# Dilated attention in a two-layer decoder trunk: queries sorted by parity and residue, scores in pieces of 32 queries

## The chip, the cores and the metric

The kernel runs on one core of a Trainium2 chip. The metric is the device time of one execution in microseconds (us); lower is better.

## The reference

Two layers, each: x plus half a SwiGLU network; then a mixing block of HGRN2 (a gated linear recurrence) and dilated attention, both gated and added to x; then x plus half of another SwiGLU network. The sequence has 256 positions, the model 1024 features. All is fp32. What the change touches is the attention:

```python
SEQ = 256
ATT_PATTERNS = ((128, 1), (512, 4), (2048, 16))   # window, dilation of three groups
ATT_HEADS = 4
ATT_DH = 128
...
s = jnp.einsum('bhrnqd,bhrnkd->bhrnqk', qb, kb) * (dh ** -0.5)   # keys of the query's residue alone
s = jnp.where(mask, s, -jnp.inf)
lse = jax.nn.logsumexp(s, axis=-1)
p = jnp.exp(s - lse[..., None])
...
alpha = jax.nn.softmax(jnp.stack(lses, axis=0), axis=0)
o_b = jnp.einsum('gbht,gbhtd->bthd', alpha, jnp.stack(outs, axis=0)).reshape(b, t, ATT_OUT)
```

Query t attends to keys t - j x dilation within the window, in each of three groups. The groups are merged by the weights of their denominators, which is one softmax over the keys of all three groups together, with each group's own queries, keys and values. With dilation 4 a query meets only keys of its residue modulo 4, with dilation 16 of its residue modulo 16.

## The kernel before, in words

**Weights.** Nearly all of the work is products with weights. Each weight tile comes from HBM as fp32, is split on ScalarE (ACT, L211 or L258) and VectorE (DVE, L212 or L259) into a high and a low part, and TensorE (PE) multiplies high by high, high by low and low by high. `full` (L240) and `mm_feat` (L216) have the weights as stationary operand and move 256 positions; `wide` (L246) and `mm_half` (L230) have 128 positions as stationary operand and move 512 weight columns, once for positions 0 to 127 and once for 128 to 255. Split weight tiles have four buffers.

**Attention** (`attn`, L550). For three groups g, `qk_unit` makes normalised and rotated queries and keys, transposed to `qT` and `kT` (features on partitions, positions along them). `v_unit` (L594) makes the values `V` (positions on partitions in two halves) by `wide`, scaled by `rstd`, the norm's factor per position. Then, for each of 4 heads:

- `soft` (L599) goes through two halves c of the queries, 128 each; I call this a half head. Scores (L612) are plain fp32 matmuls, one for each group: 128 queries stationary, 128 keys moving for c = 0 and 256 for c = 1, into one PSUM bank or two. DVE adds the mask and takes the maximum (L614), ACT exponentiates with the sum (L617), DVE takes the reciprocal (L618) and scales (L619). PE transposes the probabilities in blocks of 128x128 (L623): 3 for c = 0, 6 for c = 1, and DVE copies them out (L624) to `PT0` (keys 0 to 127) and `PT1` (keys 128 to 255, for the second half of the queries).
- `weigh` (L627) multiplies values by probabilities into one PSUM tile, 3 matmuls of 256 queries (L631) and 3 of 128 (L633), and ACT and DVE split the result into two parts (L635, L636), the input of the next weight product.

**What sets the order.** `HEAD_ORDER` (L26) interleaves scores, values and weighting in the program. A scheduler in the tile framework then puts the instructions of each engine into a fixed order when the program is built, so weight matmuls of other stages stand between a half head's scores and its transposes. Each engine runs its own list strictly in that order. Small PSUM results share three banks.

**Another user of the same form.** HGRN2's `gram` (L432) multiplies with only 32 columns of the array: four neighbouring matmuls write four different strips of 32 PSUM partitions, by `tile_position`. `square_sums` (L275) takes the squares' sums over features by matmuls with a column of ones (L287), and `norm_scale` (L297) makes `rstd` from them.

From the first transposes of probabilities to the last weighting, layer 0 takes 427 to 491 us of the span, layer 1 1123 to 1187.

Of the kernel before, what the change touches and what calls it, by code (L numbers as in the profile page):

```python
# [9 lines left out]
F32 = mybir.dt.float32  # L10
F32R = mybir.dt.float32r
I32 = mybir.dt.int32
AF = mybir.ActivationFunctionType
# [3 lines left out]
T = 256  # L17
# [5 lines left out]
CW = 512  # L23
# [9 lines left out]
LINE = 512  # L33
MOVE, STAND = 32, 108
EPS = 1e-6
BIG = 3.0e38
MIX_HQ, MIX_HF, MIX_HI, MIX_HG = 0, 1024, 2048, 3072
MIX_AQ, MIX_AK, MIX_AV, MIX_GA, MIX_GB = 4096, 5632, 7168, 8704, 9728
# [2 lines left out]
C_ID = 0  # L41
C_COS = 128
C_SIN = 384
C_M0 = 640
C_M1 = C_M0 + 384
C_LV = C_M1 + 768
C_END = C_LV + 8 * 32


def _shape_constants():  # L50

    c = np.zeros((128, C_END), np.float32)
    c[:, C_ID:C_ID + 128] = np.eye(128, dtype=np.float32)
    inv = (10000.0 ** (-np.arange(0, 128, 2) / 128.0)).astype(np.float32)
    ang = np.arange(T, dtype=np.float32)[:, None] * inv[None, :]
    cos, sin = np.cos(ang.astype(np.float64)), np.sin(ang.astype(np.float64))
    for h in range(2):
        r = slice(h * 128, (h + 1) * 128)
        c[:, C_COS + h * 128:C_COS + (h + 1) * 128] = np.concatenate([cos[r], cos[r]], 1)
        c[:, C_SIN + h * 128:C_SIN + (h + 1) * 128] = np.concatenate([-sin[r], sin[r]], 1)  # L60
    for h, base, n in ((0, C_M0, 128), (1, C_M1, 256)):
        t = np.arange(128)[:, None] + 128 * h
        s = np.arange(n)[None, :]
        for g, (w, d) in enumerate(((128, 1), (512, 4), (2048, 16))):
            ok = (t - s >= 0) & (t - s <= w) & ((t - s) % d == 0)
            c[:, base + g * n:base + (g + 1) * n] = np.where(ok, 0.0, -BIG)
    s = (np.arange(128) % 32)[:, None]
    t = np.arange(32)[None, :]
    lv = [(s // 4 == t // 4) & (t - s == d) for d in range(4)]
    lv += [(s // 16 == t // 16) & (t // 4 - s // 4 == d) for d in range(1, 4)]  # L70
    lv += [(s < 16) & (t >= 16)]
    for i, m in enumerate(lv):
        c[:, C_LV + i * 32:C_LV + (i + 1) * 32] = m
    return c


@with_exitstack
def trunk(ctx, tc, x, ffn1_norm, ffn1_w_in, ffn1_w_out, mix_norm, w_in, lb_logits, out_norm,
# [38 lines left out]
    rstd = const.tile([128, 2], F32, name="rstd")  # L117
# [4 lines left out]
    m0 = ct[:, C_M0:C_M0 + 384]  # L122
    m1 = ct[:, C_M1:C_M1 + 768]

    def lv_f(i):
        return ct[:, C_LV + i * 32:C_LV + (i + 1) * 32]
# [100 lines left out]
                nc.tensor.matmul(o, hi[:, f], al, start=False, stop=False, skip_group_check=True)  # L227
                nc.tensor.matmul(o, lo[:, f], ah, start=False, stop=e, skip_group_check=True)  # L228

    def mm_half(o, h, wu, ah, al, k0, nk, first, last):  # L230

        t = slice(h * 128, (h + 1) * 128)
        for k in range(nk):
            hi, lo = wu[k]
            s, e = first and k == 0, last and k == nk - 1
            nc.tensor.matmul(o, ah[:, k0 + k, t], hi, start=s, stop=False, skip_group_check=True)  # L236
            nc.tensor.matmul(o, ah[:, k0 + k, t], lo, start=False, stop=False, skip_group_check=True)  # L237
            nc.tensor.matmul(o, al[:, k0 + k, t], hi, start=False, stop=e, skip_group_check=True)  # L238

    def full(w, col, ap, nk=KD, step=0):  # L240
        wu = unit(w, 0, nk, col, step)
# [1 line left out]
        mm_feat(ps, wu, ap, 0, nk, True, True)  # L243
        return ps

    def wide(w, col, ap, nk=KD):  # L246

        ah, al = halves(ap)
        ps = [ps_mm.tile([128, 512], F32, name="mm") for _ in range(2)]
        for k0 in range(0, nk, 4):  # L250
            raw = wts.tile([128, KD, CU], F32, name="raw", bufs=RB).rearrange("p (k a) c -> p k (a c)", a=2)
            n = min(4, nk - k0)
            nc.sync.dma_start(raw[:, :n, :],
                              w[k0 * 128:(k0 + n) * 128, col:col + CW].rearrange("(k p) c -> p k c", p=128))
            for a in range(0, n, 2):
                hi, lo = weight_parts(MOVE, CW)
                r = raw[:, a:a + 2, :]
                nc.scalar.activation(hi, r, AF.Copy)  # L258
                nc.vector.tensor_sub(lo, r, hi.bitcast(F32))  # L259
                wu = [(hi[:, k, :], lo[:, k, :]) for k in range(2)]  # L260
                for h in range(2):
                    mm_half(ps[h], h, wu, ah, al, k0 + a, 2, k0 + a == 0, k0 + a + 2 == nk)
        return ps

    def v2(a):
# [9 lines left out]
    def square_sums(work):  # L275
        acc = work.tile([128, 2, T], F32, name="nacc", bufs=1)
        for q in range(KD // 2):
            if q == 0:
                nc.scalar.activation(acc, xT[:, 0:2, :], AF.Square)
            else:  # L280
                sq = work.tile([128, 2, T], F32, name="nsq", bufs=2)
                nc.scalar.activation(sq, xT[:, 2 * q:2 * q + 2, :], AF.Square)
                nc.vector.tensor_add(acc, acc, sq)
        nc.vector.tensor_add(acc[:, 0, :], acc[:, 0, :], acc[:, 1, :])
        ps = bank("tr")
        for h in range(2):
            nc.tensor.matmul(ps[:, h:h + 1], acc[:, 0, h * 128:(h + 1) * 128], ones[:, 0:1], start=True, stop=True)  # L287
        return ps[:, 0:2]

    def square_sums_x(work, x0):  # L290
        ss = work.tile([128, 2], F32, name="nss", bufs=1)
# [3 lines left out]
        return ss  # L295

    def norm_scale(work, ss):  # L297
        ms = work.tile([128, 2], F32, name="nms", bufs=1)
        nc.vector.tensor_scalar(ms, ss, 1.0 / D, EPS, op0=OP.mult, op1=OP.add)
        nc.gpsimd.tensor_tensor(rstd, ms, mhalf[:, 0:2], op=OP.pow)  # L300
# [249 lines left out]
    def attn(ap, l, obh, obl):  # L550
# [41 lines left out]
                nc.vector.tensor_copy(dst[:, g, hs, :], pt)  # L592

        def v_unit(g):  # L594
            ps = wide(w, MIX_AV + g * CW, xp)
            for c in range(2):
                nc.scalar.activation(V[:, g, c, :], ps[c], AF.Copy, scale=rstd[:, c:c + 1])

        def soft(h):  # L599
            PT0 = ap.tile([128, 3, T], F32, name="pt0", bufs=2)  # L600
            PT1 = ap.tile([128, 3, 128], F32, name="pt1", bufs=2)
            for c in range(2):
                n = 128 * (c + 1)
                S = ap.tile([128, 3, n], F32, name=f"as{c}", bufs=2)
                mx = ap.tile([128, 4], F32, name=f"amx{c}", bufs=2)
                t = slice(c * 128, (c + 1) * 128)
                mk = (m0, m1)[c].rearrange("p (g s) -> p g s", g=3)
                prev = BIG
                for i, gs in enumerate([(0, 1, 2)] if c == 0 else [(0, 1), (2,)]):
                    sp_ = bank()[:, :len(gs) * n].rearrange("p (g s) -> p g s", s=n)  # L610
                    for j, g in enumerate(gs):
                        nc.tensor.matmul(sp_[:, j, :], qT[:, g, h, t], kT[:, g, h, 0:n], start=True, stop=True)  # L612
                    r = slice(gs[0], gs[-1] + 1)
                    nc.vector.tensor_tensor_reduce(out=S[:, r, :], in0=sp_, in1=mk[:, r, :], scale=-1.0, scalar=prev,  # L614
                                                   op0=OP.add, op1=OP.min, accum_out=mx[:, i:i + 1])
                    prev = mx[:, i:i + 1]
                nc.scalar.activation(S, S, AF.Exp, scale=-1.0, bias=prev, accum_out=mx[:, 2:3])  # L617
                nc.vector.reciprocal(mx[:, 3:4], mx[:, 2:3])  # L618
                nc.vector.tensor_scalar(S, S, mx[:, 3:4], None, op0=OP.mult)  # L619
                for s in range(c + 1):  # L620
                    pt = bank()[:, :384].rearrange("p (g t) -> p g t", g=3)
                    for g in range(3):
                        nc.tensor.transpose(pt[:, g, :], S[:, g, s * 128:(s + 1) * 128], ident)  # L623
                    nc.vector.tensor_copy(PT0[:, :, t] if s == 0 else PT1, pt)  # L624
            return PT0, PT1

        def weigh(h, PT0, PT1):  # L627
            v = slice(h * 128, (h + 1) * 128)
            po = bank()[:, :T]
            for g in range(3):  # L630
                nc.tensor.matmul(po, V[:, g, 0, v], PT0[:, g, :], start=(g == 0), stop=False, skip_group_check=True)  # L631
            for g in range(3):
                nc.tensor.matmul(po[:, 128:256], V[:, g, 1, v], PT1[:, g, :], start=False, stop=(g == 2),  # L633
                                 skip_group_check=True)
            nc.scalar.activation(obh[:, h, :], po, AF.Copy)  # L635
            nc.vector.tensor_sub(obl[:, h, :], po, obh[:, h, :].bitcast(F32))  # L636

        for g in range(3):
            qk_unit(0, MIX_AQ, qT, g)
# [10 lines left out]
    def mix(l):  # L650
        norm_parts(1, l)
        with ExitStack() as es:
            mp = es.enter_context(tc.tile_pool(name="mix", bufs=1))
            pf0 = full(w_in[l], MIX_HF, xp)
            with tc.tile_pool(name="norm", bufs=2) as work:
                norm_scale(work, square_sums(work))
# [90 lines left out]
```

## Time and profile before

| | |
|---|---|
| median of 3 runs | 1410.68 us (1410.31 to 1411.54) |
| the profiled execution | 1410.22 us |
| its span, first to last instruction | 1408.4 us |
| granted TensorE clock, mean | 0.998 |
| busy: PE, PEld, DVE, ACT, POOL | 1398.9, 1324.4, 992.7, 790.2, 92.5 us |
| DMA queue of the weights, share of 16 engines | 53.8% |

PE is TensorE's matmuls, PEld its weight loads, which overlap them. In a row of a group stand the line, engine and operation, output<-input, shapes and count, then busy us and mean ns of one, then idle time before it and what ended that. In a timeline row stand the start, the length up to the last end, and the group; `x6` is six neighbouring instructions. A plain fp32 matmul stands as two instructions. A matmul's own time is longer than the distance to the next one's start, since matmuls are pipelined.

### The profile page before, as it was taken

To read this page: it belongs to the slowest core of one execution; us is meant where nothing else is said; L and a number is where in the kernel's file an instruction comes from. 1 tells how busy PE (TensorE), PEld (TensorE's weight loads), DVE (VectorE), ACT (ScalarE), POOL (GpSimd) and SP (SyncE) were. 2 spreads that over 40 slices of the span, in tenths; PEclk is the share of its full clock that TensorE was granted. 3 is DMA by queue.
4 is the path that set the end of the run, shared out by engine and by line. 5 is a ranking of instruction groups with operands and counts; after the bars stand their busy time and mean duration, and the time that the engine had idled before them with its cause. 6 is when DMAs were issued, how large, how long until landed. Compare 5 with 4: busy or idle time off the path is not lost.

```text
span 1408.4 us, 26973 instructions
## 1 busy us (share of the span) xinstructions
PE 1398.9 (99%) x11362; PEld 1324.4 (94%) x11362; DVE 992.7 (70%) x1452; ACT 790.2 (56%) x1259; POOL 92.5 (7%) x86
## 2 busy tenths in 40 slices
PE   8999999999999999999999999999999999999998
PEld 7999998998889999999999999988988899999987
DVE  6766569876986687666567665798779766777653
ACT  6544457667864565454454544666577646555442
POOL 0000010003510000000000000100035000000000
PEclk9999999999999999999999999999999999999999
DMA  9665564445554365655556555554454534665652
GB/s 303 199 195 187 187 210 151 150 150 180 179 180 150 120 198 192 200 189 193 196 187 202 183 191 195 183 174 139 159 181 155 196 119 143 202 202 188 195 180 104
DMA packets 215882, 253.17 MB, mean 180 GB/s; under 512 B 4225, under 2 KB 182609, under 8 KB 215761
## 3 DMA queue, kind: packets, MB, share of 16 engines
q1 hardware_dynamic: 215584, 251.38, 53.8%
q8 instruction: 89, 1.46, 0.4%
q14 instruction: 33, 0.26, 0.1%
q10 hardware_dynamic: 176, 0.07, 0.0%
HBM read 250.39 MB, written 1.05 MB: 179 GB/s over the span
## 4 chain that ended last, share of the span: by engine, by line
PE 99%; ACT 0%; DMA 0%; DVE 0%; issue 0%
PE mm L226 23%; PE mm L228 23%; PE mm L227 22%; PE mm L236 8%; PE mm L238 8%; PE mm L237 8%; PE sm L432 1%; PE sm L612 1%; PE tr L591 1%; PE sm L631 1%; PE sm L623 1%; PE sm L633 0%; PE sm L497 0%; PE sm L542 0%; PE sm L524 0%; PE sm L523 0%
## 5 line engine op out<-in xcount | busy, mean ns | idle before, releaser
L211 ACT ACTIVATE wp<-raw 128x1024 fp32r<-128x1024 f32 (+1 forms) x354 | 367.8, 1041 | 395.9 <-PE mm L228 309.6
L212 DVE TENSOR_TENSOR wp<-raw,wp 128x1024 fp32r<-128x1024 f32 (+1 forms) x354 | 424.3, 1200 | 230.0 <-ACT wp L211 227.5
L226 PE MATMUL mm<-xp,wp 128*128 128x256 f32 x1920 | 532.3, 278 | 1.8 <-ACT wp L211 1.8
L228 PE MATMUL mm<-xp,wp 128*128 128x256 f32 x1920 | 532.9, 278 | 0.2 <-DVE wp L212 0.2
L227 PE MATMUL mm<-xp,wp 128*128 128x256 f32 x1920 | 532.7, 278 | 0.0
L226 PEld LDWEIGHTS mm<-xp,wp 128*128 128x128 f32 x1920 | 360.9, 188 | 3.3 <-ACT wp L211 2.1
L228 PEld LDWEIGHTS mm<-xp,wp 128*128 128x128 f32 x1920 | 361.1, 188 | 1.1 <-DVE wp L212 0.4
L227 PEld LDWEIGHTS mm<-xp,wp 128*128 128x128 f32 x1920 | 361.0, 188 | 0.6
L259 DVE TENSOR_TENSOR wp<-raw,wp 128x1024 fp32r<-128x1024 f32 x126 | 155.4, 1234 | 64.2 <-ACT wp L258 63.4
L258 ACT ACTIVATE wp<-raw 128x1024 fp32r<-128x1024 f32 x126 | 133.2, 1063 | 80.5 <-PE mm L238 46.3
L236 PE MATMUL mm<-wp,xp 128*128 128x512 f32 x416 | 164.8, 396 | 0.0
L238 PE MATMUL mm<-wp,xp 128*128 128x512 f32 x416 | 163.4, 393 | 0.0
L237 PE MATMUL mm<-wp,xp 128*128 128x512 f32 x416 | 162.9, 392 | 0.0
L226 PE MATMUL mm<-hp,wp 128*128 128x256 f32 x528 | 145.7, 276 | 0.0
L227 PE MATMUL mm<-hp,wp 128*128 128x256 f32 x528 | 145.7, 276 | 0.0
L228 PE MATMUL mm<-hp,wp 128*128 128x256 f32 x528 | 145.7, 276 | 0.0
L226 PEld LDWEIGHTS mm<-hp,wp 128*128 128x128 f32 x528 | 99.1, 188 | 0.0
L228 PEld LDWEIGHTS mm<-hp,wp 128*128 128x128 f32 x528 | 99.1, 188 | 0.0
L227 PEld LDWEIGHTS mm<-hp,wp 128*128 128x128 f32 x528 | 99.1, 188 | 0.0
L238 PEld LDWEIGHTS mm<-wp,xp 128*128 128x128 f32 x416 | 78.2, 188 | 16.2
L236 PEld LDWEIGHTS mm<-wp,xp 128*128 128x128 f32 x416 | 78.2, 188 | 15.4
L237 PEld LDWEIGHTS mm<-wp,xp 128*128 128x128 f32 x416 | 78.2, 188 | 15.3
(194 smaller groups left out, 1741.0 us busy)
## 6 DMA issues: line engine op xcount, KB each, us to landing
raw<-in_ffn_w_in_dram SPq DMA_DIRECT2D x87, 1024.0 KB, 5.1
raw<-in_w_in_dram SPq DMA_DIRECT2D x84, 1024.0 KB, 4.9
raw<-in_ffn_w_out_dram SPq DMA_DIRECT2D x34, 1024.0 KB, 5.1
raw<-in_ffn_w_out_dram SPq DMA_DIRECT2D x12, 768.0 KB, 4.4
raw<-in_w_branch_a_dram SPq DMA_DIRECT2D x8, 1024.0 KB, 5.1
raw<-in_w_out_dram SPq DMA_DIRECT2D x8, 1024.0 KB, 5.7
raw<-in_w_branch_b_dram SPq DMA_DIRECT2D x8, 512.0 KB, 3.4
x<-in_x_dram SPq DMA_DIRECT2D x4, 256.0 KB, 3.9
```

Source lines behind the costliest of these rows:

```text
L211: nc.scalar.activation(hi[:, :n, :], r, AF.Copy)
L212: nc.vector.tensor_sub(lo[:, :n, :], r, hi[:, :n, :].bitcast(F32))
L226: nc.tensor.matmul(o, hi[:, f], ah, start=s, stop=False, skip_group_check=True)
L227: nc.tensor.matmul(o, hi[:, f], al, start=False, stop=False, skip_group_check=True)
L228: nc.tensor.matmul(o, lo[:, f], ah, start=False, stop=e, skip_group_check=True)
L236: nc.tensor.matmul(o, ah[:, k0 + k, t], hi, start=s, stop=False, skip_group_check=True)
L237: nc.tensor.matmul(o, ah[:, k0 + k, t], lo, start=False, stop=False, skip_group_check=True)
L238: nc.tensor.matmul(o, al[:, k0 + k, t], hi, start=False, stop=e, skip_group_check=True)
L258: nc.scalar.activation(hi, r, AF.Copy)
L259: nc.vector.tensor_sub(lo, r, hi.bitcast(F32))
L432: nc.tensor.matmul(p[32 * b:32 * b + 32, c * n:(c + 1) * n], kk[:, o], mov(o), start=True, stop=True, tile_position=(0, 32 * b))
L591: nc.tensor.transpose(pt[:, h, c * 128:(c + 1) * 128], z[:, c, 2 * a + h, :], ident)
```

## The change

A half head c now holds the queries of one parity, t mod 2 = c, in four pieces of 32, each with one residue modulo 8 (`rho`). Its scores are 12 matmuls of 32 array columns, one for each piece and group, written to the piece's own strip of PSUM partitions. A piece meets all 256 keys in the first group, the 64 keys of its residue modulo 4 in the second and the 32 keys of its residue modulo 8 in the third; the masks, in the new order, leave the right ones. Queries are read with a step of 8 elements, keys with a step of 1, 4 and 8. The whole half head fits one bank of 352 columns. The probabilities of the first group are scaled where they are (256 columns); those of the second and third go to blocks of 128x128 that are zero elsewhere (two DVE operations, four ACT copies). Four transposes follow, one copy of 512 columns, and `weigh` has 2 matmuls of 256 queries and 4 of 128. The values of the second and third group are made with positions sorted by parity, so the activations are read with a step of 2 in `mm_half`, and `rstd` gets two more columns. The result is written back to the order of positions by ACT and DVE. The blocks are zeroed on POOL once in a layer.

```diff
-        t = slice(h * 128, (h + 1) * 128)
+    def half_of(a, h, turned):
+
+        return a.rearrange("p (t c) -> p c t", c=2)[:, h, :] if turned else a[:, h * 128:(h + 1) * 128]
...
         for k in range(nk):
+            ahk, alk = (half_of(a[:, k0 + k, :], h, turned) for a in (ah, al))
...
+            nc.tensor.matmul(o, ahk, hi, start=s, stop=False, skip_group_check=True)
+            nc.tensor.matmul(o, ahk, lo, start=False, stop=False, skip_group_check=True)
+            nc.tensor.matmul(o, alk, hi, start=False, stop=e, skip_group_check=True)
...
-        for h in range(2):
-            nc.tensor.matmul(ps[:, h:h + 1], acc[:, 0, h * 128:(h + 1) * 128], ones[:, 0:1], start=True, stop=True)
+        for i in range(4 if turned else 2):
+            nc.tensor.matmul(ps[:, i:i + 1], half_of(acc[:, 0, :], i % 2, i > 1), ones[:, 0:1], start=True, stop=True)
...
+            ps = wide(w, MIX_AV + g * CW, xp, turned=g > 0)
...
+        def every(a, i, n):
+            return a.rearrange("p (t n) -> p n t", n=n)[:, i, :]
+
+        blocks = [[ap.tile([128, 2, 128], F32, name=f"ab{c}{i}", bufs=1) for i in range(2)] for c in range(2)]
+        for a in blocks[0] + blocks[1]:
+            nc.gpsimd.memset(a, 0.0)
...
-                        nc.tensor.matmul(sp_[:, j, :], qT[:, g, h, t], kT[:, g, h, 0:n], start=True, stop=True)
+                for g, n in enumerate((1, 4, 8)):
+                    for j in range(4):
+                        rho = c + 2 * (j // 2) + 4 * (j % 2)
+                        nc.tensor.matmul(sp_[32 * j:32 * j + 32, at:at + T // n], every(qT[:, g, h, :], rho, 8),
+                                         every(kT[:, g, h, :], rho % n, n), start=True, stop=True,
+                                         tile_position=(0, 32 * j))
+                    at += T // n
+                nc.vector.tensor_tensor_reduce(out=S, in0=sp_[:, 0:SC], in1=masks[c], scale=-1.0, scalar=BIG,
+                                               op0=OP.add, op1=OP.min, accum_out=mx[:, 0:1])
+                nc.scalar.activation(S, S, AF.Exp, scale=-1.0, bias=mx[:, 0:1], accum_out=mx[:, 2:3])
                 nc.vector.reciprocal(mx[:, 3:4], mx[:, 2:3])
-                nc.vector.tensor_scalar(S, S, mx[:, 3:4], None, op0=OP.mult)
+                nc.vector.tensor_scalar(S[:, 0:T], S[:, 0:T], mx[:, 3:4], None, op0=OP.mult)
+                for j in range(4):
+                    p = slice(32 * j, 32 * j + 32)
+                    a = j // 2 + 2 * (j % 2)
+                    if j % 2 == 0:
+                        p2 = slice(32 * j, 32 * j + 64)
+                        nc.vector.tensor_scalar(every(B[p2, 0, :], j // 2, 2), S[p2, T:T + 64], mx[p2, 3:4], None,
+                                                op0=OP.mult)
+                    nc.scalar.activation(every(B[p, 1, :], a, 4), S[p, T + 64:SC], AF.Copy, scale=mx[p, 3:4])
+                pt = bank().rearrange("p (g t) -> p g t", g=4)
+                for i in range(4):
+                    src = S[:, i * 128:(i + 1) * 128] if i < 2 else B[:, i - 2, :]
+                    nc.tensor.transpose(pt[:, i, :], src, ident)
+                nc.vector.tensor_copy(PT[:, :, t], pt)
...
+            for s in range(2):
+                nc.tensor.matmul(po, V[:, 0, s, v], PT[:, s, :], start=(s == 0), stop=False, skip_group_check=True)
+            for g in (1, 2):
+                for c in range(2):
+                    t = slice(c * 128, (c + 1) * 128)
+                    nc.tensor.matmul(po[:, t], V[:, g, c, v], PT[:, 1 + g, t], start=False, stop=(g == 2 and c == 1),
+                                     skip_group_check=True)
```

**Where instructions move.** First PE, in layer 0, at the end of head 0 and the start of head 1. Before, the six transposes (`as` is the probabilities, `ct` holds the identity) and the next half head's scores (`kT`, `qT`) stand as two closed groups between weight matmuls (`pp`, `wp`):

```order
L228 MATMUL mm<-pp,wp 128x256
L226 MATMUL mm<-pp,wp 128x256
L623 MATMUL sm<-ct,as_4571 128x128 x6
L612 MATMUL sm<-kT,qT 128x128 x3
L227 MATMUL mm<-pp,wp 128x256
```

Now, at the same place (`ab` is the blocks, rows of 32 are the strips of the array):

```order
L229 MATMUL mm<-pp,wp 128x256
L230 MATMUL mm<-pp,wp 128x256
L649 MATMUL sm<-ct,as_4596 128x128 x2
L629 MATMUL sm<-kT,qT 32x256
L649 MATMUL sm<-ct,ab_3838 128x128 x2
L629 MATMUL sm<-kT,qT 32x256 x3
L629 MATMUL sm<-kT,qT 32x64 x4
L629 MATMUL sm<-kT,qT 32x32 x4
L231 MATMUL mm<-pp,wp 128x256
```

One of the four pieces of the first group moved between the transposes, alone. It is so in five of the eight half heads of each layer; in the first one the third group's pieces stand apart, 100 rows behind the others, and in two the scores stand together.

Then ACT, from the exponentials of head 0's second half to those of head 1 (`av` is the values, `wp<-raw` the split of weights). Before:

```order
L617 ACTIVATE as_4571,amx_4572<-as_4571,amx_4572 128x768
L597 ACTIVATE av<-mm,rstd 128x512
L211 ACTIVATE wp<-raw 128x1024 x2
L617 ACTIVATE as_4799,amx_4800<-as_4799,amx_4800 128x384
L211 ACTIVATE wp<-raw 128x1024 x2
L617 ACTIVATE as_4814,amx_4815<-as_4814,amx_4815 128x768
```

Now:

```order
L635 ACTIVATE as_4596,amx_4597<-as_4596,amx_4597 128x352
L606 ACTIVATE av<-mm,rstd 128x512
L645 ACTIVATE ab_3838<-as_4596,amx_4597 32x32 x4
L606 ACTIVATE av<-mm,rstd 128x512
L214 ACTIVATE wp<-raw 128x1024 x2
L635 ACTIVATE as_4832,amx_4833<-as_4832,amx_4833 128x352
L645 ACTIVATE ab_3837<-as_4832,amx_4833 32x32 x4
L214 ACTIVATE wp<-raw 128x1024 x2
L635 ACTIVATE as_4863,amx_4864<-as_4863,amx_4864 128x352
L645 ACTIVATE ab_3839<-as_4863,amx_4864 32x32 x4
```

The four copies into the blocks stand behind each exponential, most often directly, ahead of the weight splits that followed it before.

More of the change, by code (lines that the diff above doesn't have):

```diff
@@ L35 @@
 EPS = 1e-6
+SC = T + 64 + 32
 BIG = 3.0e38
@@ L58, in _shape_constants @@
         r = slice(h * 128, (h + 1) * 128)
[L59 to L66, printed above, removed]
+        tab[:, C_COS + h * 128:C_COS + (h + 1) * 128] = np.concatenate([cos[r], cos[r]], 1)
+        tab[:, C_SIN + h * 128:C_SIN + (h + 1) * 128] = np.concatenate([-sin[r], sin[r]], 1)
+    row = np.arange(128)
+    for c in range(2):
+        rho = c + 2 * (row // 64) + 4 * (row // 32 % 2)
+        t = (rho + 8 * (row % 32))[:, None]
+        at = C_MK + c * SC
+        for n, (w, d) in zip((1, 4, 8), ((128, 1), (512, 4), (2048, 16))):
+            gap = t - (rho[:, None] % n + n * np.arange(T // n)[None, :])
+            ok = (gap >= 0) & (gap <= w) & (gap % d == 0)
+            tab[:, at:at + T // n] = np.where(ok, 0.0, -BIG)
+            at += T // n
     s = (np.arange(128) % 32)[:, None]
@@ L121, in trunk @@
     sin_t = ct[:, C_SIN:C_SIN + 256].rearrange("p (h d) -> p h d", h=2)
-    m0 = ct[:, C_M0:C_M0 + 384]
-    m1 = ct[:, C_M1:C_M1 + 768]
+    masks = [ct[:, C_MK + c * SC:C_MK + (c + 1) * SC] for c in range(2)]
     def lv_f(i):
@@ L228, in mm_feat, with mm_half @@
                 nc.tensor.matmul(o, lo[:, f], ah, start=False, stop=e, skip_group_check=True)
-    def mm_half(o, h, wu, ah, al, k0, nk, first, last):
-        t = slice(h * 128, (h + 1) * 128)
+    def half_of(a, h, turned):
+        return a.rearrange("p (t c) -> p c t", c=2)[:, h, :] if turned else a[:, h * 128:(h + 1) * 128]
+    def mm_half(o, h, wu, ah, al, k0, nk, first, last, turned=False):
         for k in range(nk):
+            ahk, alk = (half_of(a[:, k0 + k, :], h, turned) for a in (ah, al))
             hi, lo = wu[k]
             s, e = first and k == 0, last and k == nk - 1
-            nc.tensor.matmul(o, ah[:, k0 + k, t], hi, start=s, stop=False, skip_group_check=True)
-            nc.tensor.matmul(o, ah[:, k0 + k, t], lo, start=False, stop=False, skip_group_check=True)
-            nc.tensor.matmul(o, al[:, k0 + k, t], hi, start=False, stop=e, skip_group_check=True)
+            nc.tensor.matmul(o, ahk, hi, start=s, stop=False, skip_group_check=True)
+            nc.tensor.matmul(o, ahk, lo, start=False, stop=False, skip_group_check=True)
+            nc.tensor.matmul(o, alk, hi, start=False, stop=e, skip_group_check=True)
     def full(w, col, ap, nk=KD, step=0):
@@ L244, in full, with wide @@
         return ps
-    def wide(w, col, ap, nk=KD):
+    def wide(w, col, ap, nk=KD, turned=False):
         ah, al = halves(ap)
@@ L261, in wide @@
                 for h in range(2):
-                    mm_half(ps[h], h, wu, ah, al, k0 + a, 2, k0 + a == 0, k0 + a + 2 == nk)
+                    mm_half(ps[h], h, wu, ah, al, k0 + a, 2, k0 + a == 0, k0 + a + 2 == nk, turned)
         return ps
@@ L273, in norm_parts, with square_sums @@
                                            xh[:, k, :].bitcast(F32), op0=OP.mult, op1=OP.subtract)
-    def square_sums(work):
+    def square_sums(work, turned=False):
         acc = work.tile([128, 2, T], F32, name="nacc", bufs=1)
@@ L285, in square_sums @@
         ps = bank("tr")
-        for h in range(2):
-            nc.tensor.matmul(ps[:, h:h + 1], acc[:, 0, h * 128:(h + 1) * 128], ones[:, 0:1], start=True, stop=True)
-        return ps[:, 0:2]
+        for i in range(4 if turned else 2):
+            nc.tensor.matmul(ps[:, i:i + 1], half_of(acc[:, 0, :], i % 2, i > 1), ones[:, 0:1], start=True, stop=True)
+        return ps[:, 0:4 if turned else 2]
     def square_sums_x(work, x0):
@@ L297, in norm_scale @@
     def norm_scale(work, ss):
-        ms = work.tile([128, 2], F32, name="nms", bufs=1)
+        n = ss.shape[1]
+        ms = work.tile([128, n], F32, name="nms", bufs=1)
         nc.vector.tensor_scalar(ms, ss, 1.0 / D, EPS, op0=OP.mult, op1=OP.add)
-        nc.gpsimd.tensor_tensor(rstd, ms, mhalf[:, 0:2], op=OP.pow)
+        nc.gpsimd.tensor_tensor(rstd[:, 0:n], ms, mhalf[:, 0:n], op=OP.pow)
         pr = bank("tr")
@@ L594, in v_unit @@
         def v_unit(g):
[L595 removed]
+            o = 2 if g else 0
+            ps = wide(w, MIX_AV + g * CW, xp, turned=g > 0)
             for c in range(2):
[L597 removed]
+                nc.scalar.activation(V[:, g, c, :], ps[c], AF.Copy, scale=rstd[:, o + c:o + c + 1])
+        def every(a, i, n):
+            return a.rearrange("p (t n) -> p n t", n=n)[:, i, :]
+        blocks = [[ap.tile([128, 2, 128], F32, name=f"ab{c}{i}", bufs=1) for i in range(2)] for c in range(2)]
@@ L599, in soft @@
+        for a in blocks[0] + blocks[1]:
+            nc.gpsimd.memset(a, 0.0)
         def soft(h):
-            PT0 = ap.tile([128, 3, T], F32, name="pt0", bufs=2)
-            PT1 = ap.tile([128, 3, 128], F32, name="pt1", bufs=2)
+            PT = ap.tile([128, 4, T], F32, name="pt", bufs=2)
             for c in range(2):
-                n = 128 * (c + 1)
-                S = ap.tile([128, 3, n], F32, name=f"as{c}", bufs=2)
+                S = ap.tile([128, SC], F32, name=f"as{c}", bufs=2)
+                B = blocks[c][h % 2]
@@ L605, in soft @@
                 mx = ap.tile([128, 4], F32, name=f"amx{c}", bufs=2)
                 t = slice(c * 128, (c + 1) * 128)
[L607 to L624, printed above, removed]
@@ L628, in weigh @@
+                pt = bank().rearrange("p (g t) -> p g t", g=4)
[3 more added lines that the diff above has]
+                nc.vector.tensor_copy(PT[:, :, t], pt)
+            return PT,
+        def weigh(h, PT):
             v = slice(h * 128, (h + 1) * 128)
             po = bank()[:, :T]
-            for g in range(3):
-                nc.tensor.matmul(po, V[:, g, 0, v], PT0[:, g, :], start=(g == 0), stop=False, skip_group_check=True)
@@ L632, in weigh @@
[L632 to L636, printed above, removed]
+            for s in range(2):
+                nc.tensor.matmul(po, V[:, 0, s, v], PT[:, s, :], start=(s == 0), stop=False, skip_group_check=True)
+            for g in (1, 2):
+                for c in range(2):
+                    t = slice(c * 128, (c + 1) * 128)
+                    nc.tensor.matmul(po[:, t], V[:, g, c, v], PT[:, 1 + g, t], start=False, stop=(g == 2 and c == 1),
+                                     skip_group_check=True)
@@ L638, in attn @@
+            for c in range(2):
+                src = po[:, c * 128:(c + 1) * 128].rearrange("p (b u f) -> p b u f", b=2, u=2)
+                dh, dl = (o[:, h, :].rearrange("p (f u b c) -> p c b u f", u=2, b=2, c=2)[:, c] for o in (obh, obl))
+                nc.scalar.activation(dh, src, AF.Copy)
+                nc.vector.tensor_sub(dl, src, dh.bitcast(F32))
         for g in range(3):
@@ L655, in mix @@
             with tc.tile_pool(name="norm", bufs=2) as work:
-                norm_scale(work, square_sums(work))
+                norm_scale(work, square_sums(work, True))
             oap = parts_of(mp, KD, "pp")
```

20 lines of the change are left out of this document (10 added, 10 removed).

## Prediction

> **What bounds the kernel now.** I read the page's busy times first, then its chain of waits, then the busy time by stretches of the span.
>
> ```profile
> span 1408.4 us, 26973 instructions
> PE 1398.9 (99%) x11362; PEld 1324.4 (94%) x11362; DVE 992.7 (70%) x1452; ACT 790.2 (56%) x1259; POOL 92.5 (7%) x86
> PE 99%; ACT 0%; DMA 0%; DVE 0%; issue 0%
> 432.00:500.00 68.00, 68.00 (x558) 66.88 (x557) 44.80 (x76) 35.80 (x47) 0.00 (x0) 1.00 0.38 124
> 1090.00:1185.00 95.00, 95.00 (x645) 87.53 (x644) 67.71 (x113) 54.95 (x86) 3.29 (x2) 1.00 0.44 148
> ```
>
> TensorE is busy from end to end, and the chain that ended last is 99% PE. The last two rows are stretches that hold most of the attention of layer 0 and of layer 1 (columns: length, then PE, PEld, DVE, ACT and POOL busy, granted clock, DMA): PE never idles there and its clock is full, while DVE has a third and ACT nearly half of its time free. So the change is worth what it adds to or takes from PE's own stream. A busy PE says nothing of rate, so I take prices from the distance between starts in the timeline, below for the last transposes of one head half and the weighting of a head.
>
> ```profile
> 449.88 0.28 PE L227 MATMUL mm<-pp,wp 128*128 128x256 f32 x1
> 449.99 0.28 PE L228 MATMUL mm<-pp,wp 128*128 128x256 f32 x1
> 450.11 0.82 PE L623 MATMUL sm<-ct,as 128*128 128x128 f32 x6
> 450.76 1.46 PE L631 MATMUL sm<-pt,av 128*128 128x256 f32 x6
> 452.06 0.83 PE L633 MATMUL sm<-pt,av 128*128 128x128 f32 x6
> 452.65 0.36 PE L226 MATMUL mm<-pp,wp 128*128 128x256 f32 x1
> 452.85 0.28 PE L227 MATMUL mm<-pp,wp 128*128 128x256 f32 x1
> ```
>
> A weight matmul of 256 columns comes every 0.113 us (449.88 to 449.99 to 450.11). Three plain fp32 matmuls stand as six instructions, so each is two passes. A transpose costs (450.76 - 450.11) / 6 = 0.109, a pass of 256 columns (452.06 - 450.76) / 6 = 0.217, a pass of 128 columns (452.85 - 452.06 - 0.113) / 6 = 0.113. The scores (L612) have the same two shapes and I give them the same prices.
>
> **What the change takes away.** Scores of a head: 3 matmuls of 128 columns and 3 of 256, so 6 x 0.113 + 6 x 0.217 = 1.98 us; 8 heads in two layers: 15.8 us. Transposes: 8 for 9 a head, 8 x 0.109 = 0.9 us less. Weighting: 4 passes of 256 and 8 of 128 (1.77 us) in place of 6 and 6 (1.98), 8 x 0.21 = 1.7 us less.
>
> **What it adds: scores in pieces.** There are now 16 half heads, each with 4 pieces x 3 groups, 32 columns of the array wide, moving 256, 64 and 32 keys. The kernel has such matmuls already, in HGRN2 (L432): four neighbours on four column strips.
>
> ```profile
> 218.76 0.28 PE L227 MATMUL mm<-xp,wp 128*128 128x256 f32 x1
> 218.97 1.08 PE L432 MATMUL sm<-W,hk 128*32 128x128 f32 x32
> 219.98 0.39 PE L228 MATMUL mm<-xp,wp 128*128 128x256 f32 x1
> 220.20 0.28 PE L226 MATMUL mm<-xp,wp 128*128 128x256 f32 x1
> 276.57 0.28 PE L227 MATMUL mm<-xp,wp 128*128 128x256 f32 x1
> 276.78 0.46 PE L432 MATMUL sm<-hqq,s4k 128*32 128x32 f32 x32
> 277.17 0.39 PE L228 MATMUL mm<-xp,wp 128*128 128x256 f32 x1
> 277.39 0.28 PE L226 MATMUL mm<-xp,wp 128*128 128x256 f32 x1
> L432 PE MATMUL sm<-W,hk 128*32 128x128 f32 x256 | 9.7, 276 | 0.0
> L432 PE MATMUL sm<-hqq,s4k 128*32 128x32 f32 x256 | 3.7, 198 | 0.0
> ```
>
> The 32 passes of 128 columns last 1.08 us, of which the last one's own time is 0.28: 0.80 us for seven steps of four passes, less some 0.04 of start, so 0.109 us for four. That is the price of one full-width pass of 128: four strips run side by side. For 32 columns, (0.46 - 0.20 - 0.03) / 7 = 0.034. Between the two, 64 columns are 0.059; 256 columns I take at the full-width 0.217. A half head is then 2 x (0.217 + 0.059 + 0.034) = 0.62 us, and 16 of them 9.9 us.
>
> **The boundaries.** Going into strips and back costs. From 218.76 to 220.20 are 1.44 us: two weight matmuls (0.23), eight steps of 0.109 (0.87), and 0.34 left over. From 276.57 to 277.39: 0.82 - 0.23 - 0.27 = 0.32. So 0.33 for each group of strip matmuls between full-width ones: the entry waits, and the first weight matmul behind has lost the cover for its weight load (0.22 to the next in place of 0.113). The Trainium skill says the same ("TensorEngine Tiling (Array Packing)", Key Properties): changing the tiling mode drains TensorE. It gives no time, so by it alone the sum would stand at the first rival's figure plus a drain without a price for every group.
>
> In the changed order such groups are not 16 but 28: in five of the eight half heads of a layer, one piece is issued alone between transposes, and in the first the third group comes apart, since its keys come later. The same pattern of one strip matmul between transposes stands in layer 1 of the old trace:
>
> ```profile
> 971.09 0.33 PE L542 MATMUL sm<-ct,hog 128*128 128x128 f32 x1
> 971.35 0.41 PE L432 MATMUL sm<-W,hk 128*32 128x128 f32 x2
> 971.68 0.33 PE L542 MATMUL sm<-ct,hog 128*128 128x128 f32 x1
> ```
>
> From transpose to transpose 0.59 us: 0.109 for it, two passes of 0.109, and 0.27 for the boundary. So ten boundaries at 0.27 and eighteen at 0.33 make 8.6 us. And the ten pieces that go alone run their 2 x 0.217 beside nothing, while the other three still take as long as four: 10 x 0.43 = 4.3 us.
>
> Scores so far: 9.9 + 8.6 + 4.3 - 15.8 = +7.0 us.
>
> **Steps in memory.** Queries are read 8 elements apart as stationary operand, keys of the second group 4 apart and of the third 8 apart as moving operand, and the turned values' activations 2 apart. No TensorE operand steps in the trace of before. ACT's do:
>
> ```profile
> L424 ACT ACTIVATE X<-W 128x512 f32<-128x512 f32 x8 | 9.3, 1166 | 2.9 <-DVE W L401 2.0 <-DVE s4B L415 0.9
> L424 ACT ACTIVATE hqq<-X 128x512 f32<-128x512 f32 x8 | 5.0, 625 | 3.2 <-DVE X L401 3.1
> L412 ACT ACTIVATE s1k<-hk 128x128 f32<-128x128 f32 x8 | 3.4, 430 | 0.0
> L412 ACT ACTIVATE s4k<-s1k 128x128 f32<-128x128 f32 x8 | 2.4, 303 | 0.1
> ```
>
> The first of each pair takes single elements 513 or 4 apart, the second runs of four: (1166 - 625) / 512 = 1.06 ns and (430 - 303) / 128 = 0.99 ns more per element. Ends for TensorE: nothing (a plain fp32 pass takes 0.217 / 256 = 0.85 ns a column, which may hide a step), or ACT's 1 ns for the elements of all four strips in turn, 4 x (64 + 32) x 2 passes x 16 = 12.3 us. I take ACT's 1 ns once for the 64 + 32 columns that the strips read side by side, as in the nearest row: 2 x 96 ns = 0.19 us a half head, +3.1 us. The skill's rule on SBUF ("SBUF — State Buffer", Specifications) is that a 16-byte line wants two hits for full bandwidth; the ACT pairs agree with it; by it the second and third group pay, and the fourth rival falls.
>
> The turned values are 192 matmuls with 512 moving columns, whose weight load must fit under the matmul before it:
>
> ```profile
> 393.13 0.39 PE L238 MATMUL mm<-wp,xp 128*128 128x512 f32 x1
> 393.36 0.39 PE L236 MATMUL mm<-wp,xp 128*128 128x512 f32 x1
> L236 PEld LDWEIGHTS mm<-wp,xp 128*128 128x128 f32 x416 | 78.2, 188 | 15.4
> ```
>
> A matmul comes every 0.23 us and the load takes 0.188, so 0.04 is free. With a line shared by two elements the load grows by perhaps a seventh of ACT's 1 ns a column, 0.02 us: hidden. I count zero; without that cover it is the third rival. By the same page's rule two hits a line are enough, so it also says zero.
>
> **Small edits.** Two more sums of squares a layer, each two passes. The row below gives 0.125 us a pass, eight passes: +1.0 us.
>
> ```profile
> L287 PE MATMUL tr<-ones,nacc 128*128 128x1 f32 x20 | 2.5, 228 | 0.0
> ```
>
> Masks of another layout, four memsets on an idle POOL, the power of four columns: off the path, zero. What covers the new ACT and DVE work is the time between scores and transposes:
>
> ```profile
> 436.39 0.72 PE L612 MATMUL sm<-kT,qT 128*128 128x128 f32 x5
> 438.23 0.54 DVE L614 CUSTOM_DVE_ANT_0 as<-sm,ct 128x384 f32<-128x384 f32 x1
> 438.82 0.62 ACT L617 ACTIVATE as<-as,amx 128x384 f32<-128x384 f32 x1 [2.68 <-DVE amx L614]
> 439.71 0.16 DVE L618 RECIPROCAL amx<-amx 128x1 f32<-128x1 f32 x1
> 439.91 0.42 DVE L619 TENSOR_SCALAR as<-as,amx 128x384 f32<-128x384 f32 x1
> 442.54 0.49 PE L623 MATMUL sm<-ct,as 128*128 128x128 f32 x3
> L467 ACT ACTIVATE AT<-ha 32x128 f32<-32x128 f32 x32 | 9.8, 308 | 8.3 <-DVE ha L439 7.3 <-DVE s4S L414 0.8
> ```
>
> The probabilities are ready at 440.33, and PE comes for them at 442.54: 2.2 us of cover. The four copies into the blocks now stand behind the exponential on ACT, wait there for the reciprocal, hold up the next weight cast, and end 4 x 0.31 = 1.2 us after it, at about 441.1. ACT had just waited 2.68 us for work, so the cast has room. Zero; if a cast gets between, up to 1 us a half head (second rival).
>
> **The sum.** +7.0 - 0.9 - 1.7 + 1.0 + 3.1 = +8.5 us. The profiled execution took 1410.22 us (span 1408.4), the median of three runs is 1410.68: 1418.7 by the one, 1419.2 by the other. I say 1419.0.
>
> **Rivals.**
> 1. *Faster: the boundaries are hidden among long passes.* The 28 edges of strip groups cost nothing where a pass lasts 0.217 us, time enough for a weight load of 0.188. Then, with steps free, 9.9 + 4.3 - 15.8 - 0.9 - 1.7 + 1.0 = -3.2 us: 1407.5. It decides where a boundary is 3.2 / 28 = 0.11 us. Against it: no group of strips in the trace pays under 0.27. Chance 0.04.
> 2. *The chain over ACT and DVE becomes late.* Transposes of the blocks then wait in most half heads, 16 x 0.5 us more: 1427. For it: ACT is strictly in order and now waits on DVE twice in a half head. Against it: the 2.2 us. Chance 0.1.
> 3. *The turned weight loads stick out.* At ACT's full 1.06 ns a column they take 0.188 + 0.136 = 0.324 us, 0.095 over the matmul's pace, 192 times: +18 us, 1437. Chance 0.07.
> 4. *Steps cost TensorE nothing.* 1419.0 - 3.1 = 1415.9. For it: the fp32 pass is half as fast as the weight matmuls' (0.217 against 0.113 for 256). Chance 0.22.
> 5. *The pieces don't run side by side with 256 columns*, so that the change doesn't do what it says: 16 x 3 x 0.43 = +21 us, 1440. Against it: the 128-column steps. Chance 0.03.
>
> The forecast itself has 0.54. The range goes from 1413 (steps free, boundaries at 0.23) to 1427 (the second rival, or most of the way to the steps' upper end). 0.2% is 2.8 us, about what a measurement of this kernel can tell from no change: faster by more 0.04, within it 0.07 (steps free and boundaries a third cheaper), slower 0.89.
>
> **What would show it.** In the profile after: PE still 99% busy; the starts within a half head's group 0.2 us apart for four passes of 256; two separate groups per half head in five of eight; about 0.3 us left over at each; the 64- and 32-key steps at about 0.12 and 0.07 us for four if reads step at ACT's price, at 0.06 and 0.03 if they step free. The prediction is wrong if the weight loads of the turned values show more than 0.22 us, if PE shows idle time before the transposes of the blocks, or if boundaries fall below 0.2 us.

## The result and the profile after

| | before | after |
|---|---|---|
| median (range), 6 runs each | 1411.11 us (1409.84 to 1411.72) | 1419.78 us (1418.48 to 1420.34) |
| profiled execution, span | 1410.22, 1408.4 us | 1418.48, 1416.7 us |

The ratio is 1.0062, with a 95% interval from 1.0052 to 1.0072: slower by 0.6%, 8.7 us, where 1419.0 us was forecast.

The page of the profile after has the same picture as before, only longer. Its span, busy times and chain:

```profile
span 1416.7 us, 27633 instructions
PE 1407.5 (99%) x11650; PEld 1323.3 (93%) x11650; DVE 997.0 (70%) x1468; ACT 807.6 (57%) x1327; POOL 91.6 (6%) x94
PE 99%; ACT 0%; DMA 0%; DVE 0%; issue 0%
```

The two stretches with the attention, columns as in the prediction:

```profile
432.00:500.00 68.00, 68.00 (x635) 62.95 (x634) 45.20 (x83) 42.56 (x77) 0.00 (x0) 1.00 0.37 118
1090.00:1185.00 95.00, 95.00 (x735) 82.06 (x734) 65.10 (x119) 59.14 (x116) 3.45 (x3) 1.00 0.45 147
```

And all that PE waited for on other engines in the whole span (us in total, times, longest):

```profile
PE sm L168 <- DMA x<-in_x_dram: 4.0, 1, 4.0
PE mm L229 <- ACT wp L214: 1.7, 1, 1.7
```

PE grew by 8.6 us of busy time and the span by 8.3. ACT grew by 17 us, and PE did not wait for it: both waits of PE lie at the start of the program, none in the attention. In the attention PE is never idle, but its weight loads (PEld) cover less of it than before, 62.95 of 68 us against 66.88, as one would expect of more boundaries. The 8.3 us are inside PE's own stream, so I read them there. First a half head whose scores are split by the transposes, then one whose 24 passes stand together (12 matmuls of two passes; a timeline row bears the shape of its first):

```profile
436.49 0.28 PE L230 MATMUL mm<-pp,wp 128*128 128x256 f32 x1
436.61 0.38 PE L649 MATMUL sm<-ct,as 128*128 128x128 f32 x2
436.92 0.65 PE L629 MATMUL sm<-kT,qT 128*32 128x256 f32 x2
437.50 0.44 PE L649 MATMUL sm<-ct,ab 128*128 128x128 f32 x2
437.87 1.02 PE L629 MATMUL sm<-kT,qT 128*32 128x256 f32 x22
438.82 0.38 PE L231 MATMUL mm<-pp,wp 128*128 128x256 f32 x1
439.04 0.28 PE L229 MATMUL mm<-pp,wp 128*128 128x256 f32 x1
...
454.46 1.03 PE L629 MATMUL sm<-kT,qT 128*32 128x256 f32 x24
455.42 0.38 PE L231 MATMUL mm<-pp,wp 128*128 128x256 f32 x1
455.64 0.28 PE L229 MATMUL mm<-pp,wp 128*128 128x256 f32 x1
```

Together, the 24 passes take 0.96 us to the next weight matmul; split, two and twenty-two take 0.58 and 0.95, so the 22 gain nothing from the two that ran ahead. After each group the next two weight matmuls stand 0.22 apart. I measured every block with scores in both traces in the same way: from the start of the matmul ahead of it to the start of the second weight matmul behind it, less 0.113 for each weight matmul that this counts in (0.2275 where it moves 512 columns), and less the transposes and the weighting at their prices. The scores took 16.1 us before and 26.7 after; the rounding of the prices leaves about 0.1 us open. Below, "by the blocks" means this sum.

### The profile page after: what moved, and what is told of

Its sections match the earlier page's. It is cut to its first block, busy times and chain, and to the rows that moved or that the text cites. A ratio compares the mean times of both kernels' runs of the same rounds, so it can differ in the third digit from the quotient of the medians.

```text
span 1416.7 us, 27633 instructions
## 1 busy us (share of the span) xinstructions
PE 1407.5 (99%) x11650; PEld 1323.3 (93%) x11650; DVE 997.0 (70%) x1468; ACT 807.6 (57%) x1327; POOL 91.6 (6%) x94
## 4 chain that ended last, share of the span: by engine, by line
PE 99%; ACT 0%; DMA 0%; DVE 0%; issue 0%
PE mm L231 23%; PE mm L229 22%; PE mm L230 22%; PE mm L243 8%; PE mm L245 8%; PE mm L244 8%; PE sm L629 2%; PE sm L440 1%; PE tr L599 1%; PE sm L649 1%; PE sm L661 1%; PE sm L657 0%; PE sm L505 0%; PE sm L550 0%; PE sm L533 0%; PE sm L532 0%
```

## The experiments

There were two sessions. Experiments 1, 4, 6 and 7 were timed beside the kernel before, which had 1410.60 us there. The changed kernel itself and experiments 2, 3 and 5 were timed in the other session, where the kernel before had 1410.71 us. Differences below are to the changed kernel's 1419.1 us unless another base is named.

**The base.** No edit.

> The changed kernel itself, as the base for the three runs beside it on this chip: 1419.8 us by every theory.

Measured: 1419.10 us (1418.77 to 1420.23), ratio to before 1.0061 (1.0049 to 1.0074).

**1. Scores of a whole head together.** The two loops over half heads are parted:

```diff
...
+            banks = []
             for c in range(2):
                 sp_ = bank()
...
+                banks.append(sp_)
+            for c in range(2):
...
+                sp_ = banks[c]
                 nc.vector.tensor_tensor_reduce(out=S, in0=sp_[:, 0:SC], in1=masks[c], ...
...
```

> The scores of both half heads of a head are issued before the softmax of either. The program's order then has 12 strip groups in place of 28 and no piece of 256 keys alone between transposes; pieces, steps, transposes and weighting are as in the changed kernel. Theory (boundaries cost about 0.3 each, lone pieces 0.43 each): 16 x 0.29 + 10 x 0.43 = 8.9 us less than the changed kernel, about 1411 us. Rival (boundaries are hidden, only lone pieces cost): 4.3 us less, 1415.5. Rival (neither costs; the pieces themselves are slow): no change. If the transposes now come too early for the softmax, PE shows idle time ahead of them and the gain is smaller.

Measured: 1411.09 us (1410.00 to 1412.02, 11 runs), ratio to before 1.0003 (0.9994 to 1.0012): 8.0 us less. The same 384 passes, with the same steps, and the kernel is back at the time of before. From the same weight matmul at about 56 us to the last one, the traces differ by 9.0 us; the medians also hold the start of the program, which differs by up to 1.5 us among the traces of the changed kernel and its variants. Two half heads in one group, from the timeline:

```profile
433.58 0.40 PE L245 MATMUL mm<-wp,xp 128*128 128x512 f32 x1
433.90 1.83 PE L627 MATMUL sm<-kT,qT 128*32 128x256 f32 x48
435.67 0.39 PE L229 MATMUL mm<-pp,wp 128*128 128x256 f32 x1
435.89 0.28 PE L230 MATMUL mm<-pp,wp 128*128 128x256 f32 x1
```

48 passes in 1.77 us, 0.89 for a half head. Boundaries and lone pieces together are the cost, and the rival by which neither costs falls. This run alone doesn't part the two.

**2. Short groups first.**

```diff
-                for g, n in enumerate((1, 4, 8)):
+                for g, n, at in ((2, 8, T + 64), (1, 4, T), (0, 1, 0)):
...
-                    at += T // n
```

> The groups of a half head go in the order 32, 64, 256 keys; the pieces themselves, transposes and weighting stay. The program's order then has 32 strip groups in place of 28, and what stands alone between transposes is one to four short pieces (32 or 64 keys) and never one of 256 keys. Theory (a lone piece costs its own length, a boundary about 0.27 to 0.3): ten long lone pieces fewer, -4.3; some ten short ones instead, +1.0; four boundaries more, +1.1: 2.2 us less than the changed kernel. Rival (lone pieces cost nothing, since the idle strip starts its next piece at once, and the boundaries are dearer instead): 1 to 2 us more. Rival (boundaries are free, lone pieces cost): 3.3 us less.

Measured: 1417.94 us (1416.83 to 1418.80), ratio to before 1.0050 (1.0038 to 1.0063): 1.2 us less, and the two intervals overlap, so the medians alone decide little. By its blocks in the trace the attention takes 1.96 us less than in the base, near the theory's 2.2; the rivals' 3.3 less and 1 to 2 more both fall. The two traces also differ by 0.6 us, the other way, in the first 58 us of the span, where nothing was edited.

**3. Without the copies into the blocks.**

```diff
-                    nc.scalar.activation(every(B[p, 1, :], a, 4), S[p, T + 64:SC], AF.Copy, scale=mx[p, 3:4])
```

> The four ACT copies into the blocks are dropped; left out: the third group's probabilities, which stay zero. The order on TensorE is as in the changed kernel but for the second half head of each layer, whose scores now stand together (two boundaries and two lone pieces fewer in all). Theory (ACT and DVE are off the path): -2 x 0.7 = 1.4 us less than the changed kernel, all of it at those two half heads. Rival (the second of the prediction, the chain over ACT and DVE is late): several us less, and shorter times at the other half heads too.

Measured: 1418.56 us (1417.38 to 1419.09), ratio to before 1.0055 (1.0041 to 1.0069): 0.5 us less, inside the noise. By the blocks it is 1.46 us less, all at the two half heads that now stand together; each of the others that are split still takes 2.33 us with its four transposes, as in the base. The copies on ACT don't set the time, and PE waits for neither ACT nor DVE in the attention of the changed kernel: the second rival falls.

The second half head of layer 0 exists now in three forms with the same work of four transposes and 24 passes. First the changed kernel, a piece of 256 keys alone between transposes:

```profile
428.60 0.38 PE L649 MATMUL sm<-ct,as 128*128 128x128 f32 x2
428.82 0.27 PE L649 MATMUL sm<-ct,ab 128*128 128x128 f32 x1
429.02 0.65 PE L629 MATMUL sm<-kT,qT 128*32 128x256 f32 x2
429.60 0.33 PE L649 MATMUL sm<-ct,ab 128*128 128x128 f32 x1
429.86 1.02 PE L629 MATMUL sm<-kT,qT 128*32 128x256 f32 x22
430.82 0.51 PE L245 MATMUL mm<-wp,xp 128*128 128x512 f32 x1
```

Then short groups first, where all four strips of the 32-key pieces stand apart and no strip runs alone:

```profile
427.37 0.38 PE L647 MATMUL sm<-ct,as 128*128 128x128 f32 x2
427.58 0.27 PE L647 MATMUL sm<-ct,ab 128*128 128x128 f32 x1
427.79 0.34 PE L628 MATMUL sm<-kT,qT 128*32 128x32 f32 x8
428.06 0.33 PE L647 MATMUL sm<-ct,ab 128*128 128x128 f32 x1
428.32 0.89 PE L628 MATMUL sm<-kT,qT 128*32 128x64 f32 x16
429.14 0.51 PE L244 MATMUL mm<-wp,xp 128*128 128x512 f32 x1
```

And without the copies, nothing apart:

```profile
429.15 0.38 PE L648 MATMUL sm<-ct,as 128*128 128x128 f32 x2
429.37 0.38 PE L648 MATMUL sm<-ct,ab 128*128 128x128 f32 x2
429.68 1.03 PE L629 MATMUL sm<-kT,qT 128*32 128x256 f32 x24
430.63 0.50 PE L245 MATMUL mm<-wp,xp 128*128 128x512 f32 x1
```

From the first transpose to the weight matmul: 2.22, 1.77 and 1.48 us. One more boundary is 1.77 - 1.48 = 0.29; a lone long piece on top of it is 2.22 - 1.77 = 0.45. The prediction had 0.27 and 0.43. The other order of the groups alone matters little: by the blocks, a half head that stands together behind the weighting takes 1.15 us in the base and 1.14 with short groups first.

**4. No steps.**

```diff
-                        nc.tensor.matmul(sp_[32 * j:32 * j + 32, at:at + T // n], every(qT[:, g, h, :], rho, 8),
-                                         every(kT[:, g, h, :], rho % n, n), start=True, stop=True,
+                        nc.tensor.matmul(sp_[32 * j:32 * j + 32, at:at + T // n], qT[:, g, h, 32 * j:32 * j + 32],
+                                         kT[:, g, h, 0:T // n], start=True, stop=True,
```

> The score pieces read 32 neighbouring queries and the first 256, 64 or 32 keys in place of stepped ones; the order on TensorE, the piece sizes and all else stay as in the changed kernel. Left out: which queries meet which keys. Theory (steps cost, 64 + 32 columns x 2 passes x 16 half heads at about 0.9 ns): 2.8 us less than the changed kernel, and four strips of 64 keys at about 0.06 us in place of 0.12, of 32 keys at 0.034 in place of 0.063. Rival (steps are free, the fourth rival of the prediction, and the slow 64-key pieces come from something else, say the short pieces waiting for weight loads): no change of time, steps still 0.12 and 0.06.

Measured: 1415.85 us (1415.28 to 1415.94), ratio to before 1.0036 (1.0023 to 1.0048): 3.3 us less; by the blocks of the trace 3.9. Steps cost, and the fourth rival falls.

**5. Keys without steps, queries with.**

```diff
-                                         every(kT[:, g, h, :], rho % n, n), start=True, stop=True,
+                                         kT[:, g, h, 0:T // n], start=True, stop=True,
```

> Keys are read as the first 256, 64 or 32 neighbours, queries still with their step of 8; left out: which keys a query meets. The order on TensorE is the same as in the changed kernel. Without both steps the time fell by 3 to 3.5 us. Theory (moving columns pay for the step): the same 2.8 to 3.5 us less than the changed kernel, and four strips of 64 keys at 0.06 us. Rival (the stepped loads of the queries pay, their mean was 144 ns against 109 ns without steps): no change, or under 1 us, and the loads still take 144 ns.

Measured: 1417.36 us (1416.78 to 1418.42), ratio to before 1.0048 (1.0035 to 1.0061): 1.7 us less; by the blocks 2.3. It lies between the two theories: moving columns pay, and so do the queries' loads. The half head that was shown above for the changed kernel, where its 24 passes took 0.96 us to the weight matmul, is in this run (with the row of its loads):

```profile
455.09 0.89 PE L629 MATMUL sm<-kT,qT 128*32 128x256 f32 x24
455.91 0.38 PE L231 MATMUL mm<-pp,wp 128*128 128x256 f32 x1
...
L629 PEld LDWEIGHTS sm<-kT,qT 128*32 128x32 f32 x384 | 13.2, 145 | 5.9 <-issue 3.8
```

And in the kernel without any steps:

```profile
454.81 0.81 PE L629 MATMUL sm<-kT,qT 128*32 128x256 f32 x24
455.55 0.39 PE L231 MATMUL mm<-pp,wp 128*128 128x256 f32 x1
...
L629 PEld LDWEIGHTS sm<-kT,qT 128*32 128x32 f32 x384 | 10.7, 109 | 6.5 <-issue 3.8
```

0.96, 0.82, 0.74 us: the keys' steps are 0.14 of a half head, the queries' 0.08. A load of 32 columns with a step of 8 takes 145 ns in the mean, without it 109: (145 - 109) / 32 = 1.1 ns more a column. In the starts of the traces it shows at the entry of a group (0.27 us for the first four passes, 0.24 without it) and at the 32-key passes, where the next four start 0.04 us later and each load takes 0.14 to 0.16.

**6. Values not turned.**

```diff
-            o = 2 if g else 0
-            ps = wide(w, MIX_AV + g * CW, xp, turned=g > 0)
+            o = 0
+            ps = wide(w, MIX_AV + g * CW, xp)
...
-                norm_scale(work, square_sums(work, True))
+                norm_scale(work, square_sums(work))
```

> Values are made in the order of positions and the norm sums are two in place of four; left out: the sorting of the values of the second and third group. The attention's order and matmuls stay as in the changed kernel. Theory (only the extra norm sums cost, the stepped weight loads are hidden): 0.9 us less than the changed kernel. Rival (the loads stick out a little, since the turned values' matmuls come every 0.233 us and not every 0.228): another 192 x 0.005 = 1.0, so 1.9 us less. Third rival of the prediction: 18 us less.

Measured: 1417.30 us (1416.61 to 1417.54), ratio to before 1.0046 (1.0034 to 1.0059): 1.8 us less. That is the first rival's 1.9, not the theory's 0.9. Below are two value matmuls of the changed kernel, the first and the last of 26 neighbours; then the loads of this stretch (from 407.5 to 413 us), the loads of the whole span, and the norm sums. The same of this kernel follows, with the stretch from 408 to 413.5 us:

```profile
407.42 0.40 PE L244 MATMUL mm<-wp,xp 128*128 128x512 f32 x1
...
413.25 0.40 PE L245 MATMUL mm<-wp,xp 128*128 128x512 f32 x1
...
L244 PEld LDWEIGHTS mm<-wp,xp 128*128 128x128 f32 x8 | 1.6, 196 | 0.3
...
L243 PEld LDWEIGHTS mm<-wp,xp 128*128 128x128 f32 x416 | 78.6, 189 | 15.7 <-ACT asq L578 0.4
L294 PE MATMUL tr<-ones,nacc 128*128 128x1 f32 x28 | 3.4, 236 | 0.0
```

```profile
407.95 0.40 PE L244 MATMUL mm<-wp,xp 128*128 128x512 f32 x1
...
413.64 0.39 PE L245 MATMUL mm<-wp,xp 128*128 128x512 f32 x1
...
L244 PEld LDWEIGHTS mm<-wp,xp 128*128 128x128 f32 x8 | 1.5, 188 | 0.3
...
L243 PEld LDWEIGHTS mm<-wp,xp 128*128 128x128 f32 x416 | 78.2, 188 | 15.8 <-ACT asq L578 0.4
L294 PE MATMUL tr<-ones,nacc 128*128 128x1 f32 x20 | 2.5, 228 | 0.0
```

25 steps in 5.83 us against 5.69: 0.2332 and 0.2276 us, so 0.0056 more for each of the 192 turned matmuls, 1.1 us. The norm sums are the other 0.9: the block of them takes 0.92 us in place of 0.46 once a layer, by the starts in the trace. A turned load takes 193 to 196 ns in the trace, one that isn't turned 188: it grew by 5 to 8 ns, and the pace grew by 5.6, though a load was still shorter than the time from one matmul to the next. In the group of the whole span the mean moved by 1 ns only, since most of its loads aren't turned: that row alone hides this.

**7. Parity alone, full width.** No strips and no blocks; the second and third group both meet the 128 keys of their parity, and masks leave the right ones:

```diff
...
-                for g, n in enumerate((1, 4, 8)):
-                    for j in range(4):
-                        rho = c + 2 * (j // 2) + 4 * (j % 2)
-                        nc.tensor.matmul(sp_[32 * j:32 * j + 32, at:at + T // n], every(qT[:, g, h, :], rho, 8),
-                                         every(kT[:, g, h, :], rho % n, n), start=True, stop=True,
-                                         tile_position=(0, 32 * j))
+                for g, n in enumerate((1, 2, 2)):
+                    nc.tensor.matmul(sp_[:, at:at + T // n], every(qT[:, g, h, :], c, 2),
+                                     every(kT[:, g, h, :], c % n, n), start=True, stop=True)
...
```

> The queries are sorted by parity alone: full-width matmuls of 128 queries, moving 256 keys in the first group and the 128 keys of the same parity in the second and third; no strips, no blocks, four transposes, the same cheaper weighting and turned values. Theory (strips with their boundaries are what costs, steps of two elements cost nothing): scores 16 x (2 x 0.217 + 4 x 0.113) = 14.2 us against 15.8 before, transposes -0.9, weighting -1.7, norm sums +1.0, so 3.2 us less than the kernel before, about 1407.9. Rival (a step of two costs TensorE as a step of four does, 0.9 ns a moving column: 4 x 128 x 16 columns): +7.4, so 4 us slower than before, about 1415.

Measured: 1407.40 us (1406.92 to 1409.27, 11 runs), ratio to before 0.9979 (0.9970 to 0.9988): 3.2 us faster than the kernel before, as expected, and 11.7 faster than the changed one. One half head in its timeline:

```profile
436.27 0.60 PE L631 MATMUL sm<-ct,as 128*128 128x128 f32 x4
436.71 1.07 PE L621 MATMUL sm<-kT,qT 128*128 128x256 f32 x6
437.53 0.37 PE L229 MATMUL mm<-pp,wp 128*128 128x256 f32 x1
```

Six full-width passes take 0.82 us and cover 512 columns; the 24 passes in strips take 0.96 and cover 352, with their steps and without a split. A step of two costs these passes little: the four of 128 keys stand 0.113 to 0.120 us apart in the trace, 0.111 without a step in the old scores. That the time came out as expected is in part luck: turned values cost 1.1 us here too, and slow stretches of the old kernel end that were worth 1.0 us (both below); the expectation had neither.

## Why the prediction was right, point by point

- **The bound.** PE's own stream, as said: 99% busy, and no wait in the attention. What was added there came out in the time.
- **Boundaries (8.6 us) and lone pieces (4.3).** Right: 0.29 and 0.45 us where the prediction had 0.27 and 0.43, and 8.0 us by the medians, 9.0 by the traces, where 8.9 was expected in the run that takes 16 boundaries and all lone pieces away. What a boundary's time is spent on was not taken apart. The first rival needs a boundary under 0.11.
- **Pieces side by side (9.9).** Right: 24 passes in 0.96 us, where the eight of 256 keys alone would take 1.7 one after the other. The fifth rival falls. Without steps (experiment 4), four strips take 0.216, 0.056 and 0.028 us a pass by the starts in the trace, so two passes of each are 0.60 us, where the prediction had 0.62.
- **Steps (3.1).** Right in kind, mis-sized, and incomplete: 3.9 us by the blocks, of which the keys have 2.3 and the queries' loads 1.6. The prediction priced the moving operand alone, at 3.1; for the stationary one it named the step and gave no term. Of its signs, four strips of 64 keys take 0.11 us and of 32 keys 0.06 by the starts in the trace (0.12 and 0.07 if reads step at ACT's price), and 0.06 and 0.03 in the run without steps. Scores without steps are then 26.7 - 3.9 = 22.8 us, which is the sum of the three terms above. The Trainium skill's rule of two hits for each 16-byte line ("SBUF — State Buffer", Specifications) gave the right side. The traces agree with it: steps of 4 and 8 cost the moving keys 0.14 us a half head, and a step of 2 costs a pass of 128 keys at most 0.009.
- **Turned values (zero).** The step that failed: it said that 0.02 us more for a load is hidden under 0.04 of spare time. The load grew by less, 0.005 to 0.008 us, to at most 0.196, below the 0.22 us that was named as a sign of being wrong. The pace grew all the same, by 0.0056 us, together 1.1 us: the spare time hid nothing. The third rival's mechanism exists, at a sixteenth of its 18 us. The same rule of the Trainium skill also said zero here, and is off by that much.
- **Transposes, weighting, norm sums (-0.9, -1.7, +1.0).** By the blocks -0.9, -1.7 and +0.9.
- **What had no term.** The old scores cost 16.1, not 15.8, and behind some of them the old kernel's weight matmuls ran slower, which the changed kernel's did not. From the trace of before, behind three score matmuls:

```profile
454.03 0.83 PE L612 MATMUL sm<-kT,qT 128*128 128x128 f32 x6
454.61 0.37 PE L228 MATMUL mm<-pp,wp 128*128 128x256 f32 x1
...
455.06 0.28 PE L228 MATMUL mm<-pp,wp 128*128 128x256 f32 x1
...
460.34 0.28 PE L227 MATMUL mm<-pp,wp 128*128 128x256 f32 x1
```

44 steps in 5.28 us: 0.120 and not 0.113. It goes on to the next transposes, and again for 36 steps behind 472 us; with the same in layer 1 about 1.1 us, gone in the changed kernel. It isn't tied to the old scores: in the run with whole heads, 29 steps of 0.120 us follow a lone transpose at 464.6 us. Why they keep that pace isn't settled.

So the sum by the traces is 26.7 - 16.1 - 0.9 - 1.7 + 0.9 + 1.1 - 1.1 = +8.9 us, and over the weight products from 58 us on the two traces differ by 8.9 us. The spans differ by 8.3, since the profiled execution of before took 0.6 us longer over its first 58 us. Its granted clock was 0.97 there against 1.00, but the base, at 1.00, took as long as it, so the clock isn't shown to be the reason. That the forecast of +8.5 is so close is luck, by errors that cancel: the steps and turned values that it adds were priced 1.9 us too low, and the old scores and slow stretches that it ends 1.4 us too low.

## What to carry to other kernels

A matmul that is cut into array strips to skip masked work has to pay for its entry and exit, here 0.3 us each time it is set among full-width ones. So count the groups in the order in which the instructions come out, and not in the program; here whole heads together brought back 8 us with the same arithmetic. Weigh what is left to skip against that: sorting by parity alone kept the cheaper weighting and transposes, needed no strips, and was the only form that beat the kernel before. Price a step in memory on both operands, the loads too, most of all when passes are shorter than a load.

## What the runs showed of the hardware

- TensorE's fp32 reads paid for steps of 4 and 8 elements, at a price near that of ACT in the old trace (1.0 ns an element): 0.14 us a half head for 96 keys in two passes is 0.7 ns a column, and a column of a load with a step of 8 cost 1.1 ns more. With a step of 2, a load of 128 columns took 193 to 196 ns in place of 188, and the pace of its matmuls grew by 0.0056 us, 0.04 ns a column.
- A train of full-width weight matmuls settled at 0.120 us in place of 0.113 behind three plain fp32 score matmuls, and in another run behind a lone transpose, and kept it for up to 5 us.
